# The first load of a column-mean kernel, with its 128 rows dealt to the partitions in another order

## The chip, the cores and the metric

The kernel runs on one core of one Trainium2 chip. The metric is the device time of one execution in microseconds, the median of several runs; lower is better. One profiled execution of the kernel before is at hand, with a record of each engine's instructions and of the packets that the core's 16 DMA engines moved.

## The reference

The mean over the rows of a matrix of 8192 x 8192 float32 numbers (268 MB). The result is one row of 8192 numbers.

```python
def setup_inputs():
    return {"x": np.random.randn(8192, 8192).astype(np.float32)}

def reference(x):
    return np.mean(x, axis=0)
```

## The kernel before

The 8192 rows are 64 groups of 128 rows; a group puts one row on each of the 128 partitions. They are cut into four strips of 17, 17, 15 and 15 groups (`strips`, L62). Within a strip of s groups, partition p owns the s consecutive rows that begin at row p times s of the strip. Because s is odd, a strip is s - 1 rows that are loaded in pairs, so that a partition reads 64 KB in one piece, and one row that is left, the last of the partition's s rows. The pairs stand in `pairs`, the four rows left in `singles` (L63 to L68); `rows(g)` gives one of the latter, for g from 60 to 63.

The order of the loads is written out by hand. All of them go out on one queue, SyncE's, through `load` (L51), which keeps program order. The first load is half a megabyte: columns 0 to 1023 of the row left of the first strip, 4 KB for each partition, into a small tile called `early` (L113, through `load_early`, L95). Partition p gets row 17p + 16 there. Neighbouring partitions thus read 17 rows of 32 KB apart, 544 KB, and partitions 8 apart read 4.25 MB apart.

Next come the loads of pairs, 8 MB each (`load_rows`, L73), into a ring of buffers in `bufs`: the first pair into the buffers that become the sum, then 29 more in the loop of L117. After the second turn of that loop the rest of `early`, columns 1024 to 3071 of the same 128 rows, is loaded as well (L125), again with row 17p + 16 on partition p. At the end the remaining single rows are loaded in pieces that grow smaller (L144 to L151).

VectorE adds each pair to the running sum (`add`, L78): first the two rows of a pair to one another, then that to the accumulator `acc`. The early turns add two rows at once, 16384 numbers wide. A buffer is loaded anew when the adds that read it have ended, and a no-op on ScalarE or GpSimd collects the waits ahead of an add. GpSimd adds `early` to the accumulator in two parts, in the turns of g = 24 and g = 32 (L135 to L140): columns 0 to 1023, those of the first load, and then columns 1024 to 3071.

Last, TensorE sums over the 128 partitions: a matrix product with a matrix of constants 1/8192 (`product`, L98), for the accumulator and for the rows that were never added to it, all into five PSUM banks. ScalarE and VectorE copy these out, and three small stores write the result. Since every column is summed over all partitions at the end, it doesn't matter for the sum on which partition a row stands.

Of the kernel before, what the change touches and what calls it, by code (L numbers as in the profile page):

```python
# [9 lines left out]
def kernel(  # L10
# [8 lines left out]
    P = nc.NUM_PARTITIONS  # L19
    F = 512  # L20
# [13 lines left out]
    early = sb.tile([P, E * F], f32, name="early")  # L34
# [16 lines left out]
    def load(dst, src):  # L51
        ins = tc.keep_in_program_order(nc.sync.dma_start(out=dst, in_=src)).ins  # L52
        k = len(loads)
        over = loads[k - 8:k - 6] if k >= 8 and k % 2 == 0 else []
        tc.declare_no_dep(ins, group="loads", keep=over, reason="the reader of the buffer waited")
        for o in over:
            tc.add_manual_dep(ins, o.name, sync, reason="covers the next load too")
        tc.add_to_no_dep_group("loads", ins)
        loads.append(ins)
        return ins  # L60

    strips = [17, 17, 15, 15]  # L62
# [7 lines left out]
    def rows(g):  # L70
        return singles[g - (G - 4)]

    def load_rows(g, u, n):  # L73
        return load(bufs[:, u:u + n, :], pairs[g // 2])
# [20 lines left out]
    def load_early(lo, hi):  # L95
        load(early[:, lo * F:hi * F], rows(G - 4)[:, lo * F:hi * F])
# [13 lines left out]
        )).ins  # L110

    sums2 = bufs[:, U - 2:, :]
    load_early(0, 2)  # L113
    first = [load_rows(0, U - 2, 2)]
    tc.keep_in_program_order(nc.scalar.copy(out=warm[:], in_=ones[:]))  # L115
    ahead = []
# [121 lines left out]
```

## Time and profile before

| what | value |
|---|---|
| median of 3 runs | 628.02 us (628.0 to 628.23) |
| span of the profiled execution | 626.3 us |
| data read from HBM | 268.44 MB, 429 GB/s over the span |
| VectorE busy | 527.7 us (84%), 92.2 us idle ahead of its adds |
| TensorE busy | 18.3 us (3%) |
| GpSimd busy | 7.4 us (1%) |
| SyncE's first load: issue begins, ends | 0.74 us, 1.13 us |
| VectorE's first add begins | 42.86 us |

The span runs from the first to the last instruction of the profiled execution; the time of a run is a little longer than that. SP is SyncE, DVE VectorE, ACT ScalarE, POOL GpSimd, PE TensorE; SPq is SyncE's sequencer, and L52 is line 52 of the kernel. Every load has line L52, whichever place in the kernel calls the helper, and every add L80.

A windows view gives for each stretch of time the busy time and count of PE, of its weight loads (PEld), of DVE, ACT and POOL, then the granted clock of TensorE (1.00 is full speed), the mean busy share of the 16 DMA engines, and the GB/s that they moved. The packet records of the trace give start, duration and size of each piece that a DMA engine moved; those of the first load are 128 packets of 4096 bytes, and those of the pairs 3840 packets of 65536 bytes.

### The profile page before, as it was taken

The page shows a single profiled execution, that of the slowest core. Times are in us where ns is not written, and L with a number is a line of the kernel's source. Part 1 is how long each engine was busy: PE and PEld are TensorE (multiplying, and loading weights), DVE is VectorE, ACT ScalarE, POOL GpSimd, SP SyncE. Part 2 cuts the span into 40 slices and gives each one's busy share as a digit, 9 for nine tenths or more (in the row PEclk, how much of TensorE's full clock was granted, in tenths as well). Part 3 has the DMA queues.
Part 4 walks back from the last instruction along what each step waited for, and adds up shares of the span by engine and source line. Part 5 has one row for each costly group of instructions (what it writes and reads, how often), then busy time and mean ns, then how long its engine had stood idle before and what let it go on. Part 6 is the DMA issues. An engine that isn't in the chain of part 4 may idle for free.

```text
span 626.3 us, 464 instructions
## 1 busy us (share of the span) xinstructions
PE 18.3 (3%) x120; PEld 4.6 (1%) x120; DVE 527.7 (84%) x60; ACT 3.7 (1%) x6; POOL 7.4 (1%) x8
## 2 busy tenths in 40 slices
PE   0000020000000000000000000000000000000035
PEld 0000000000000000000000000000000000000001
DVE  0028979999988998888988899988898888998895
ACT  0000000000000000000000000000000000000001
POOL 0000000000000000010000200000000000000000
PEclk9999999999999999999999999999999999999999
DMA  9999999999999999999999999999999999999997
GB/s 393 444 402 434 437 469 402 469 402 465 406 448 423 440 431 423 448 410 460 406 465 402 469 402 469 402 469 402 469 402 465 406 448 423 423 448 406 431 435 305
DMA packets 5658, 268.50 MB, mean 429 GB/s; under 512 B 636, under 2 KB 652, under 8 KB 1048
## 3 DMA queue, kind: packets, MB, share of 16 engines
q1 hardware_dynamic: 5648, 268.46, 99.2%
q8 instruction: 1, 0.02, 0.0%
q10 hardware_dynamic: 8, 0.01, 0.0%
q14 instruction: 1, 0.01, 0.0%
HBM read 268.44 MB, written 0.03 MB: 429 GB/s over the span
## 4 chain that ended last, share of the span: by engine, by line
DMA 70%; DVE 28%; PE 1%; SPq 0%; issue 0%; ACTq 0%; POOLq 0%
DMA bufs<-in_x_dram 70%; DVE bufs L80 28%; PE bank L102 1%; SPq L52 0%; ACTq L83 0%; DVE fin L192 0%; POOLq L83 0%
## 5 line engine op out<-in xcount | busy, mean ns | idle before, releaser
L80 DVE TENSOR_TENSOR bufs<-bufs 128x8192 f32<-128x8192 f32 (+4 forms) x59 | 527.4, 8939 | 92.2 <-POOLq L83 52.3
L102 PE MATMUL bank<-bufs,ones 128*32 128x512 f32 (+2 forms) x120 | 18.3, 634 | 605.0 <-DVE bufs L80 517.7
L137 POOL TENSOR_TENSOR bufs<-bufs,early 128x1024 f32<-128x1024 f32 (+1 forms) x2 | 6.8, 3416 | 350.0 <-DVE bufs L80 350.0
L102 PEld LDWEIGHTS bank<-bufs,ones 128*32 128x32 f32 x120 | 4.6, 120 | 618.5 <-issue 610.7
L182 ACT COPY bufs<-bank 128x512 f32<-128x512 f32 x3 | 1.8, 586 | 618.2 <-PE bank L102 618.2
L192 DVE COPY fin<-bank 128x128 f32<-128x128 f32 x1 | 0.3, 292 | 3.8 <-PE bank L102 3.8
L115 ACT ACT_TABLE_LOAD x1 | 1.3, 1283 | 0.7 <-PEq L222 0.7
L182 ACT COPY fin<-bank 128x384 f32<-128x384 f32 x1 | 0.5, 480 | 1.0 <-PE bank L102 1.0
L115 ACT COPY warm<-ones 128x32 f32<-128x32 f32 x1 | 0.2, 217 | 0.0
L40 POOL TENSOR_TENSOR ready<-ones 128x1 f32<-128x1 f32 x1 | 0.2, 192 | 0.1
L37 POOL MEMSET ones<- 128x32 f32 x1 | 0.1, 124 | 0.3 <-POOLq L222 0.3
L222 POOL MEMSET const-bfloat16-1.0<- 128x1 bf16 x1 | 0.1, 101 | 0.0
L222 POOL MEMSET const-uint8-127<- 128x1 uint8 x1 | 0.1, 101 | 0.0
L222 POOL MEMSET const-float32-0.0<- 128x1 f32 x1 | 0.1, 98 | 0.2 <-issue 0.2
L222 POOL MEMSET const-float32-1.0<- 128x1 f32 x1 | 0.1, 98 | 0.0
## 6 DMA issues: line engine op xcount, KB each, us to landing
bufs<-in_x_dram SPq DMA_DIRECT2D x2, 4096.0 KB, 16.7
bufs<-in_x_dram SPq DMA_DIRECT2D x1, 2560.0 KB
bufs<-in_x_dram SPq DMA_DIRECT2D x1, 2048.0 KB, 21.3
early<-in_x_dram SPq DMA_DIRECT2D x1, 1024.0 KB, 62.0
bufs<-in_x_dram SPq DMA_DIRECT2D x1, 1024.0 KB, 23.2
bufs<-in_x_dram SPq DMA_DIRECT2D x1, 768.0 KB, 24.7
early<-in_x_dram SPq DMA_DIRECT2D x1, 512.0 KB
bufs<-in_x_dram SPq DMA_DIRECT2D x30, 29.9
```

Of the source, the lines that this page charges most:

```text
L37: nc.gpsimd.memset(ones[:], 1.0 / M)
L40: nc.gpsimd.tensor_add(out=ready[:], in0=ones[:, 0:1], in1=ones[:, 1:2]))
L80: ins = tc.keep_in_program_order(nc.vector.tensor_add(out=dst, in0=a, in1=b)).ins
L102: return tc.keep_in_program_order(nc.tensor.matmul(out=dst, lhsT=ones[:], rhs=cols, start=start, stop=stop, tile_position=(0, 32 * q), ski ...
L115: tc.keep_in_program_order(nc.scalar.copy(out=warm[:], in_=ones[:]))
L137: ins = tc.keep_in_program_order(nc.gpsimd.tensor_add(out=acc[:, cols], in0=acc[:, cols], in1=early[:, cols])).ins
L182: return tc.keep_in_program_order(nc.scalar.copy(out=dst, in_=src)).ins
L192: ended = nc.vector.tensor_copy(out=fin[:, 3 * W:], in_=banks[4][:, :W]).ins
L222: nc = _bacc.Bacc("TRN2", target_bir_lowering=False, num_devices=1)
```

## The change

The first load takes the same columns of the same 128 rows, and its destination is the same; the order of the rows over the partitions is another. The rows of the strip are seen as 8 blocks (k) of 16 (e) times 17 (s), and the source of the load runs over e first and k second. Partition 8e + k, which had row 17(8e + k) + 16, now has row 17(16k + e) + 16. Neighbouring partitions then read 8.5 MB apart, 16 x 544 KB, and partitions 8 apart read 544 KB apart. If an engine serves 8 partitions one after the other, the 16 engines are at rows 544 KB apart at one time, and before at rows 4.25 MB apart. The second part of `early`, `load_early(2, E)`, is as it was.

```diff
     sums2 = bufs[:, U - 2:, :]
-    load_early(0, 2)
+    s = strips[0]
+    spread = x[:s * P, :].rearrange("(k e s) c -> s e k c", k=8, s=s)[s - 1]
+    load(early[:, :2 * F], spread[:, :, :2 * F])
     first = [load_rows(0, U - 2, 2)]
```

## The prediction

> **What bounds the kernel now.** I read the page first (span, DMA slices, chain of waits), then the windows view of the first microseconds, where the changed load runs, and last the window of the long middle. The page:
>
> ```profile
> span 626.3 us, 464 instructions
> DMA  9999999999999999999999999999999999999997
> ...
> q1 hardware_dynamic: 5648, 268.46, 99.2%
> ...
> DMA 70%; DVE 28%; PE 1%; SPq 0%; issue 0%; ACTq 0%; POOLq 0%
> ...
> bufs<-in_x_dram SPq DMA_DIRECT2D x30, 29.9
> ```
>
> The reader is to see that one queue, q1, keeps the 16 DMA engines at work for 99.2% of the span. VectorE stands in the chain with 28%, but section 1 of the page has it 84% busy: it follows the loads, they don't follow it. The last line says that a usual load lands 29.9 us after its issue. Such a load is 8.39 MB, which at the 432 GB/s of the middle (next fence) is 19.4 us, so it is issued some 10.5 us before its turn comes. A stream that is some tenths of a microsecond earlier or later therefore finds its issues ready, and VectorE, idle for 92.2 us in all, can follow it.
>
> The windows view; the columns that count are the last two, the DMA share and GB/s. A packet is booked whole in the window in which it starts, so shares can pass 1:
>
> ```profile
> 1.50:1.75 0.25, 0.00 (x0) 0.00 (x0) 0.00 (x0) 0.25 (x1) 0.00 (x0) 1.00 0.00 0
> 1.75:2.00 0.25, 0.00 (x0) 0.00 (x0) 0.00 (x0) 0.25 (x1) 0.00 (x0) 1.00 1.07 197
> 2.00:2.25 0.25, 0.00 (x0) 0.00 (x0) 0.00 (x0) 0.23 (x2) 0.00 (x0) 1.00 0.94 147
> 2.25:2.50 0.25, 0.00 (x0) 0.00 (x0) 0.00 (x0) 0.00 (x0) 0.00 (x0) 1.00 0.41 131
> 2.50:2.75 0.25, 0.00 (x0) 0.00 (x0) 0.00 (x0) 0.00 (x0) 0.00 (x0) 1.00 0.94 377
> 2.75:3.00 0.25, 0.00 (x0) 0.00 (x0) 0.00 (x0) 0.00 (x0) 0.00 (x0) 1.00 0.95 393
> ...
> 3.80:620.00 616.20, 14.95 (x76) 3.50 (x80) 527.38 (x59) 0.59 (x1) 6.83 (x2) 1.00 1.00 432
> ```
>
> So there is a dry stretch up to about 1.8 us, a slow start of the first load, 0.5 to 0.75 us long, and then a full stream to the end: share 1.00 from 3.80 to 620. Nothing that happens to the first load is hidden: the engines go from it straight to the next loads, and what it gains or loses moves all behind it.
>
> **The changed load now.** It is 128 rows of 4 KB, 0.52 MB, 8 packets for each of 16 engines. Packets in a window are GB/s times 0.25 us over 4096 bytes, and their time is share times 0.25 us times 16. From 1.75 to 2.50 these are 12 + 9 + 8 = 29 packets with (1.07 + 0.94 + 0.41) x 4 = 9.68 us, or 334 ns each. From 2.50 to 3.00 they are 23 + 24 = 47 packets with 1.89 x 4 = 7.56 us, 161 ns each; the trace's packet records give 159 ns for nearly all of them. The excess of the start is 9.68 - 29 x 0.159 = 5.07 us over 16 engines, **0.32 us** for each. The rows have the same distance, 4.25 MB, in the slow and in the fast part. So distance alone doesn't slow a packet; what is special at the start is that 16 engines begin within some 0.1 us of one another. In the records, 24 of the first packets took 160 to 681 ns with a mean of 374, and afterwards the engines are out of step, entering the next load between 3.39 and 3.79 us.
>
> **The change part by part.** (1) *Same work.* One load of 128 rows of 4 KB is replaced by one of the same rows. No instruction is added, removed or moved; the early tile holds the rows in another order of partitions, and each of its columns is summed over all partitions anyway. Cost of everything behind it (the GpSimd adds of 4.49 and 2.34 us, the matrix products, the last stores): nothing, as no shape and no wait differs. The GpSimd adds are at 276 and 353 us, far from the start, so no cover of theirs is touched.
>
> (2) *The slow start.* If rows 544 KB apart don't get in each other's way in the first step, the 0.32 us go; the first round of the following 64 KB packets took 2463 ns in the mean against 2422 for the rest, another 0.04 us that may go with it. Upper end of the gain: 0.36 us. Lower end: no gain, if the slow packets are what the engines' first reads cost from any rows; and below that a loss, if 544 KB is the worse distance, bounded by the same excess again, +0.32 us. The nearest row is the fast part of the same load, which shows that reads of this very kind run at 159 ns when they don't begin together, so something in the beginning together is avoidable; but nothing in the trace says that distance cures it. I take two thirds of the 0.32: **-0.21 us**.
>
> [...]
>
> (3) *Issue.* SP's first DMA instruction took 0.39 us (0.74 to 1.13) and the first packet followed 0.64 us later, at 1.77. Its source now has three dimensions instead of two. Loads of two dimensions take 0.33 to 0.44 us on SP; SP's stores with three dimensions 0.54 and 0.70. So the issue changes by -0.06 (0.33 - 0.39) to +0.31 us (0.70 - 0.39), all on the path, because the engines are dry until then; the three loads behind it on SP start later by as much, but their packets wait for this load's anyway. It is nearest to the other loads into 128 partitions: **+0.05 us**.
>
> Sum: -0.21 + 0.05 = -0.16, said as -0.2. Against the profiled execution: 626.3 - 0.2 = 626.1 us of span. The median of the runs shown, 628.02, is 1.7 us above the span, time before the first and after the last instruction that the change doesn't touch, so 628.02 - 0.2 = **627.8 us**. With the ends of both terms: -0.36 - 0.06 = -0.42 (627.6) to +0.32 + 0.31 = +0.63 (628.65).
>
> **The rivals.** *A: nothing comes of it.* The slow first packets are the price of engines that begin cold, or the engines stay in step longer and meet in the 64 KB packets of the next load instead (the worst of that first round took 2553 ns, 0.13 us more than the rest). For it: the load is fast at 4.25 MB from 2.50 us on. Against it: the first packets spread from 160 to 681 ns, like engines that queue for one thing. Time 628.0 to 628.2.
>
> *B: the rows are dealt to the engines badly* (slower). The load's two sides are now cut differently, 16 x 8 rows on one, 128 partitions on the other. If two engines write through one way into the on-chip memory, or only 8 engines get the work, the load needs the time of 16 packets in a row where it has 8: 8 x 0.159 = 1.27 us, on the path since all that follows queues behind the last engine, and with the +0.05 of the issue 1.3 us: 629.3. It decides as soon as the deal isn't one block of 8 partitions to each engine on a way of its own. For it: the stream is bound by the engines (share 1.00), so an unequal deal can't be caught up. Against it: the outermost sizes, 16 and 128, both divide by 16. If only one engine got the rows it would be 120 x 0.159 = 19 us, 647.
>
> [...] No row of this trace shows which partitions an engine has.
>
> *C: it gains more than its own load* (faster beyond the bound below). The 3840 packets of 64 KB take 2422.5 ns in the mean and 2415 at best; were the engines in a better phase for the whole run, 240 x 7.5 ns = 1.8 us of each engine would go, with 0.3 at the start 2.1 us: 625.9. Against it: the phases drift during the run (the middle stretches stand at 2418 to 2430 ns), so the start doesn't fix them.
>
> **How the numbers follow.** A measurement of this kernel can tell about 0.2%, 1.26 us, from no change: faster is below 626.8, slower above 629.3. Forecast 0.46 and A 0.26, both within 0.2%; B 0.21, of which most lies at the bound or above it; C 0.07. So faster 0.07, same 0.73, slower 0.20. The likeliest case's own range is 627.6 to 628.65. The range, 627.2 to 629.4, goes on downwards for part of C and upwards to B with eight engines or shared ways, and leaves out one engine alone and the rest of C.
>
> **What would show it.** Right: packets of the first load at about 160 to 220 ns from the start, so 1.75 to 2.50 us carries clearly more than 158 GB/s on the mean, the engines enter the next load nearer to 3.2 than to 3.57 us (their mean now), and the window 3.80 to 620 stays at 432 GB/s. A: the same low GB/s up to 2.50, or a first round of 64 KB packets over 2463 ns. Issue: SP's first instruction longer than 0.39 us and a first packet after 1.77. B: packets of the first load near 318 ns to its end, or engines that enter the next load 1.3 us apart. C: a middle above 432 GB/s. The prediction is wrong if the time leaves 627.6 to 628.65, and its reason is wrong if the start is as slow as before.

## The result, and the profile after

| | median | runs | span of the profiled execution |
|---|---|---|---|
| before | 628.23 us | 21 (627.93 to 628.81) | 626.3 us |
| changed | 629.21 us | 21 (628.83 to 629.51) | 627.5 us |

The ratio is 1.0014, with a 95% interval of 1.0008 to 1.0019: the change makes the kernel **slower**, by 0.98 us (0.16%) in the medians. That is inside the wide range, 627.2 to 629.4 us, whose upper end was set for rival B, and within 0.2% of no change. But it is on the other side of no change than the forecast, and outside the 627.6 to 628.65 us beyond which the prediction called itself wrong.

The page of the changed kernel, the same lines as of before:

```profile
span 627.5 us, 464 instructions
DMA  9999999999999999999999999999999999999997
...
q1 hardware_dynamic: 5648, 268.46, 99.2%
...
DMA 70%; DVE 28%; PE 1%; SPq 0%; issue 0%; ACTq 0%; POOLq 0%
```

On this scale nothing has changed: the same packets, the same queue busy for 99.2%, the same chain. Whatever was lost stands in stretches too short for the page. The timeline of SyncE's queue (start, duration, what) shows the first part of it:

```profile
0.74 0.70 SPq L52 DMA_DIRECT2D early<-in_x_dram  x1
1.50 1.52 SPq L52 DMA_DIRECT2D bufs<-in_x_dram  x3
```

The first load's issue takes 0.70 us where it took 0.39. The windows of the changed kernel's start (the columns as before: TensorE's clock, DMA share and GB/s come last, and a packet is booked where it starts) show the rest:

```profile
1.75:2.00 0.25, 0.00 (x0) 0.00 (x0) 0.00 (x0) 0.25 (x1) 0.00 (x0) 1.00 0.00 0
2.00:2.25 0.25, 0.00 (x0) 0.00 (x0) 0.00 (x0) 0.24 (x2) 0.00 (x0) 1.00 0.18 33
2.25:2.50 0.25, 0.00 (x0) 0.00 (x0) 0.00 (x0) 0.00 (x0) 0.00 (x0) 1.00 1.14 213
2.50:2.75 0.25, 0.00 (x0) 0.00 (x0) 0.00 (x0) 0.00 (x0) 0.00 (x0) 1.00 0.67 197
2.75:3.00 0.25, 0.00 (x0) 0.00 (x0) 0.00 (x0) 0.00 (x0) 0.00 (x0) 1.00 1.08 295
3.00:3.25 0.25, 0.00 (x0) 0.00 (x0) 0.00 (x0) 0.00 (x0) 0.00 (x0) 1.00 0.86 295
3.25:3.50 0.25, 0.00 (x0) 0.00 (x0) 0.00 (x0) 0.00 (x0) 0.00 (x0) 1.00 0.82 295
3.50:3.75 0.25, 0.00 (x0) 0.00 (x0) 0.00 (x0) 0.00 (x0) 0.00 (x0) 1.00 1.02 344
3.75:4.00 0.25, 0.00 (x0) 0.00 (x0) 0.00 (x0) 0.00 (x0) 0.00 (x0) 1.00 1.25 328
4.00:4.25 0.25, 0.00 (x0) 0.00 (x0) 0.00 (x0) 0.00 (x0) 0.00 (x0) 1.00 7.53 2441
4.25:4.50 0.25, 0.00 (x0) 0.00 (x0) 0.00 (x0) 0.00 (x0) 0.00 (x0) 1.00 3.90 1327
4.50:4.75 0.25, 0.00 (x0) 0.00 (x0) 0.00 (x0) 0.00 (x0) 0.00 (x0) 1.00 1.50 524
...
3.80:620.00 616.20, 14.78 (x67) 3.30 (x71) 526.62 (x59) 0.00 (x0) 6.83 (x2) 0.58 1.00 433
```

Three things are to be seen. The first packet comes at 2.22 us (1.77 before). The load then never reaches the 377 and 393 GB/s that it had before from 2.50 us on: it moves 197, three times 295, 344 and 328 up to 4.00. And the next load's first 64 KB packets, those that start from 4.00 to 4.75, are long: (7.53 + 3.90 + 1.50) x 4 = 51.7 us, less six packets of 4 KB at about 0.31, is 49.9 us over 16 packets, 3.1 us each, where one takes 2.42. The middle of the run is as before, 433 against 432 GB/s. TensorE's granted clock is 0.58 there against 1.00. It isn't the cause: one of the plain controls below had 0.58 too and stood within 0.04% of before, and TensorE works for 19.3 us in all.

In the packet records a loss can be summed. Two numbers tell it: the time that the small load's packets take beyond 159 ns each, over 16 engines, and the mean time beyond 2420 ns of the first 64 KB packet that each engine takes behind them.

| us for each engine | first packet at | excess of 4 KB packets | excess of next 64 KB packet | sum of both |
|---|---|---|---|---|
| before | 1.77 | 0.32 | 0.04 | 0.37 |
| changed | 2.22 | 0.60 | 0.68 | 1.28 |

So 0.45 us are lost ahead of the first packet and 0.91 in the packets, 1.36 in all. By the packet records the changed kernel has its first 9 MB 1.37 us later than before, which agrees; at the last packet of x it is 1.16 us, and the medians differ by 0.98. The 0.2 to 0.4 us that disappear on the way are taken for chance of one execution: in the profile of before the 64 KB packets between 78 and 156 us took 2429.5 ns in the mean, in the profile after 2421.5, and in three plain runs below 2419.5 to 2420.8; 32 packets of each engine, 8 ns longer, are 0.26 us. The profiled execution of the changed kernel was also the longest of its 21, at 629.51 us.

### The profile page after: what moved, and what is told of

It reads as the page before. It is cut to its first block, busy times and chain, and to the rows that moved or that the text cites. A ratio compares the mean times of both kernels' runs of the same rounds, so it can differ in the third digit from the quotient of the medians.

```text
span 627.5 us, 464 instructions
## 1 busy us (share of the span) xinstructions
PE 19.3 (3%) x120; PEld 4.8 (1%) x120; DVE 527.7 (84%) x60; ACT 3.7 (1%) x6; POOL 7.3 (1%) x8
## 3 DMA queue, kind: packets, MB, share of 16 engines
q1 hardware_dynamic: 5648, 268.46, 99.2%
## 4 chain that ended last, share of the span: by engine, by line
DMA 70%; DVE 28%; PE 1%; SPq 0%; issue 0%; ACTq 0%; POOLq 0%
DMA bufs<-in_x_dram 70%; DVE bufs L80 28%; PE bank L102 1%; SPq L52 0%; ACTq L83 0%; DVE fin L194 0%; POOLq L83 0%
## 5 line engine op out<-in xcount | busy, mean ns | idle before, releaser
L80 DVE TENSOR_TENSOR bufs<-bufs 128x8192 f32<-128x8192 f32 (+4 forms) x59 | 527.4, 8939 | 93.4 <-POOLq L83 53.9
L102 PE MATMUL bank<-bufs,ones 128*32 128x512 f32 (+2 forms) x120 | 19.3, 652 | 605.2 <-DVE bufs L80 517.4
L40 POOL TENSOR_TENSOR ready<-ones 128x1 f32<-128x1 f32 x1 | 0.2, 193 | 0.1
```

The source lines that it names most:

```text
L40: nc.gpsimd.tensor_add(out=ready[:], in0=ones[:, 0:1], in1=ones[:, 1:2]))
L80: ins = tc.keep_in_program_order(nc.vector.tensor_add(out=dst, in0=a, in1=b)).ins
L102: return tc.keep_in_program_order(nc.tensor.matmul(out=dst, lhsT=ones[:], rhs=cols, start=start, stop=stop, tile_position=(0, 32 * q), ski ...
```

## The experiments

The theory after this look: the cost comes from how the load is cut, not from where its rows lie. The cut is the sizes in which the source of a load is given: the changed one has an outermost size of 16, with 8 rows in each, and the destination has 128 partitions. The rivals: the 544 KB distance itself is bad; the slow first round is chance; the longer issue explains everything. No record here shows which partitions an engine has: where the expectations speak of an engine's block of partitions, of groups, or of ways into the partitions, that is the author's theory. All comparisons below are with the kernel before, run on the same chip beside them. The chip differs between groups of runs (the kernel before took 628.23 to 628.46 us), so two experiments are held against each other by their distances from it. The profile numbers are of one execution each.

**The changed kernel once more.**

> The changed kernel once more, so that its profile can be held against the first one: the first load's issue took 0.70 us on SP (0.39 before), the first packet stood at 2.22 us (1.77 before), and the first 64 KB packet of each engine took 3099 ns in the mean (2463 before). Theory (a three-dimensional source costs issue time and, through it, time): issue again 0.70 and first packet again 2.2, time 0.14% above before. Theory 2 (the slow first 64 KB round belongs to the change too): again near 3.1 us. Rival (that round is chance of one execution): between 2.4 and 2.6 us this time.

Measured 629.3 against 628.25 us, ratio 1.0014 (1.0005 to 1.0023). Issue 0.70 us, first packet at 2.22, excess 0.63 in the 4 KB packets, and a first 64 KB round of 2748 ns, 0.33 us more than 2420; the sum is 0.96. The round lies between the two values that were set, 3.1 us and 2.4 to 2.6. It is read here as part of the change, with a size that varies from one execution to the next (0.68 and 0.33); the next run has 0.33 again.

**Three dimensions at the old distance.**

```diff
-    load_early(0, 2)
+    far = x[:17 * P, :].rearrange("(e r) c -> e r c", r=136)[:, 16:136:16, :]
+    load(early[:, :2 * F], far[:, :, :2 * F])
```

> The first load has a source of three dimensions, 16 blocks of 8 rows, but each engine's block lies 4.25 MB from the next one's, as before; inside a block the rows are 512 KB apart. It reads 128 other rows of the strip in place of the right ones, the same bytes. If the source's dimensions are what costs: issue 0.70 us, first packet at 2.2 us, time 0.1 to 0.16% above before, as with the change. If the 544 KB distance costs and the dimensions don't: issue 0.39, time as before within 0.04%. If both: half of the way, with the first 64 KB round near 2.46 us and the issue at 0.70.

629.23 us, ratio 1.0013 (1.0004 to 1.0022), the whole cost of the change: issue 0.70, first packet at 2.22, excess 0.64 and 0.33 us. The nearness of the rows has no part in it.

**Two dimensions with near pieces.**

```diff
-    load_early(0, 2)
+    near = x[:272, :].rearrange("r c -> (r c)").rearrange("(p f) -> p f", p=P)
+    load(early[:, :2 * F], near[:, :2 * F])
```

> The first load has a source of two dimensions, 128 pieces of 4 KB that are 68 KB apart, so that partitions 8 apart read 544 KB apart; the pieces are other parts of x than the right ones, the same bytes. If the dimensions cost and the distance doesn't: issue 0.39 us, first packet at 1.77, time as before or, if the nearness relieves the first packets as the prediction had it, 0.03 to 0.05% below. If the distance costs: issue 0.39, but packets of the first load with a mean excess of 0.6 us per engine as in the change (0.32 before) and a first 64 KB round near 3.1 us, time about 0.1% above before.

628.29 us, ratio 0.9999 (0.9990 to 1.0008): no cost. Issue 0.39, first packet at 1.75. The excess is 0.44 and 0.07 us, not less than before's 0.32 and 0.04, so there is no sign of the relief either. A load whose partitions 8 apart read 544 KB apart thus gains nothing.

**The dealt load second, behind the first pair.** The edit is against the changed kernel.

```diff
-    load(early[:, :2 * F], spread[:, :, :2 * F])
     first = [load_rows(0, U - 2, 2)]
+    load(early[:, :2 * F], spread[:, :, :2 * F])
```

> The dealt load is issued second, behind the first pair of rows (8 MB), so that its longer issue stands behind other transfers. If the cost of the change is issue and cold start of the first load: the first packet (64 KB now) at 1.75 us or earlier, time no worse than before, 0 to 0.1% below, since the 0.31 us of issue and the slow 4 KB start are covered. If dealing the rows costs wherever it stands (engines sharing ways, a bad phase): time 0.05 to 0.15% above before.

629.69 against 628.25 us, ratio 1.0021 (1.0012 to 1.0030). The issue (0.69 us, from 1.18 us on) is covered there, as the load's packets pass at 22 us, and the small load doesn't meet the cold start, and it costs still more. This was the run that decided, with its control:

**The plain load second.** Lines L113 and L114 of the kernel before change places.

> The first two loads change places as in the run with the dealt load second, but the small load has its plain source of two dimensions. It is the control for that run, where the 4 KB packets went at 159 ns until 22.15 us and at 240 to 390 after, in the middle of the stream. If a badly shared way into the partitions is the cause (theory): all 128 packets here at 159 to 170 ns, the 64 KB packets behind them at 2420, and 1.2 us (0.19%) less than with the dealt load second; time about 628.4, the rest being the cold start with 64 KB packets. If small packets between large ones are slow by themselves (rival): again 250 ns and 629.7 us.

628.52 against 628.36 us, ratio 1.0004 (0.9995 to 1.0013). The windows of both where the small load passes, around 22 to 24 us, the run with the dealt load first:

```profile
22.00:22.50 0.50, 0.00 (x0) 0.00 (x0) 0.00 (x0) 0.00 (x0) 0.00 (x0) 1.00 1.22 336
22.50:23.00 0.50, 0.00 (x0) 0.00 (x0) 0.00 (x0) 0.00 (x0) 0.00 (x0) 1.00 0.95 197
23.00:23.50 0.50, 0.00 (x0) 0.00 (x0) 0.00 (x0) 0.00 (x0) 0.00 (x0) 1.00 1.03 262
```

and its plain control:

```profile
22.00:22.50 0.50, 0.00 (x0) 0.00 (x0) 0.00 (x0) 0.00 (x0) 0.00 (x0) 1.00 1.06 434
22.50:23.00 0.50, 0.00 (x0) 0.00 (x0) 0.00 (x0) 0.00 (x0) 0.00 (x0) 1.00 1.30 541
23.00:23.50 0.50, 0.00 (x0) 0.00 (x0) 0.00 (x0) 0.00 (x0) 0.00 (x0) 1.00 4.81 2073
```

At a DMA share of about 1, the dealt load moves 197 and 262 GB/s in the second and third window, the plain one 434 in the first (in the third, and partly in the second, its engines are already starting 64 KB packets). In the records, all 128 packets of the control took 159 ns. Those of the dealt load took 159 ns until 22.15 us, the first 26 of the 128, and then up to 392. From 22.2 to 23.4 us 16 to 18 of them are in flight at a time by the records, and the DMA share is about 1: all 16 engines work on the load, and each packet takes longer. Its excess is 0.79 us in these and 0.48 us in the 64 KB packets behind them, together **1.27 us** for each engine. That is just 8 packets x 0.159 us: as if the 0.52 MB went at half rate, with the backlog worked off in the packets that follow. In time the dealt load stands 1.44 us above the kernel before and the plain one 0.16 us, each on its own chip: 1.28 us apart.

**The kernel before, started late.**

```diff
+    landed(readied)
     load_early(0, 2)
```

Here `readied` is the small GpSimd addition of L40.

> The kernel before, but SP waits with the first load until GpSimd's second small instruction has ended (1.13 us), so that the issue begins about 0.42 us later. What a later start of the stream costs: if all of it passes to the end, first packet at 2.2 us and +0.42 us, 0.07%. If the issue's delay is the whole of the change's cost (rival): 0.13 to 0.15%, as the change. If a later start is partly caught up: below 0.05%.

628.63 against 628.36 us, ratio 1.0004 (0.9995 to 1.0012). The issue began at 1.16, the first packet came at 2.17, and the first 9 MB were there 0.40 us later than before. At the last packet of x it was 0.18 us. The time is 0.27 us longer, with an interval that has both no change and the whole 0.42 us in it; 0.04% is under the 0.05% that was set for a start that is partly caught up. So the medians can't tell how much of a late start passes on. Its ratio stays below the change's 1.0014, though the intervals overlap.

**Three dimensions with 128 outermost.**

```diff
-    load_early(0, 2)
+    apart = rows(G - 4).rearrange("p (j w) -> p j w", w=F)[:, 0:4:2, :]
+    load(early[:, :2 * F].rearrange("p (j w) -> p j w", w=F), apart)
```

> The first load's source has three dimensions again, but the outermost has 128 entries: each partition gets two pieces of 2 KB from its own row (the second one 2 KB further on than in the kernel before, so 512 of the early columns hold other data). Theory (what costs is the cut of the outermost dimension into 16, which hands an engine 8 partitions in a row): packets of 2 KB at 84 ns after the start, a first 64 KB round near 2.46 us; only the longer issue remains if it belongs to three dimensions as such (0.70 us, +0.3 to +0.45 us) and 0.07 us for the smaller packets, so 0.01 to 0.08% above before. Rival (three dimensions cost, however they are cut): 0.13 to 0.16% above before with a first round of 2.7 us or more.

628.45 us, ratio 1.0002 (0.9993 to 1.0011). The issue took 0.45 us, neither 0.39 nor 0.70, the 2 KB packets 84 ns once started, the first 64 KB round 2453. So a third dimension behind the 128 is worth 0.06 us of issue here; the rest came with the cut of the outermost one.

**Two halves of 64 partitions, first.**

```diff
-    load_early(0, 2)
+    tc.keep_in_program_order(nc.sync.dma_start(
+        out=early[:64, :2 * F], in_=rows(G - 4)[:64, :2 * F]))
+    load(early[64:, :2 * F], rows(G - 4)[64:, :2 * F])
```

> The first load in two, rows for partitions 0 to 63 and for 64 to 127, each plain and of two dimensions; the same bytes in the same places. Each half is dealt to 16 engines with 4 partitions, so if two engines meet at one way into the memory whenever a load covers too few different groups of partitions (theory), the packets slow to 240 to 320 ns, together with the first 64 KB round up to 1.27 us are lost for each engine, and the time is 0.1 to 0.2% above before, without any third dimension. Rival (dimensions alone): packets at 159 ns after the start and a time within 0.03% of before, the second issue being covered by the first half's packets.

631.06 us, ratio 1.0043 (1.0031 to 1.0056): a cost without a third dimension, but twice what the theory gave. In the records the excess is 0.63 us in the 4 KB packets, 0.50 in the next round and 0.48 in the round after that, and four of the engines began their first 64 KB packet only at 5.2 to 5.9 us, after 12 others at 3.7 to 4.5. Why these four waited isn't settled, and with it a part of the 2.70 us. Since the cold start is mixed in here, the halves were tried again in the middle of the stream, below.

**The second part dealt, twice the bytes.**

```diff
-                load_early(2, E)
+                s = strips[0]
+                spread = x[:s * P, :].rearrange("(k e s) c -> s e k c", k=8, s=s)[s - 1]
+                load(early[:, 2 * F:], spread[:, :, 2 * F:E * F])
```

> The first load is plain, and the second part of the early rows (1 MB, 8 KB for each partition, at about 61 us, in the middle of the stream) is dealt in 16 x 8 instead. If the deal halves the rate of the bytes that it covers (theory): 8 packets of 309 ns twice as long, 2.47 us for each engine, and 0.35 to 0.42% above before. If the cost is a fixed one of the dealt load, or belongs to the cold start (rival): 0 to 0.2%.

630.72 against 628.23 us, 2.49 us more (0.40%) where 2.47 were worked out; ratio 1.0047 (1.0035 to 1.0058), which is above the 0.35 to 0.42% that was expected: one of the six runs took 633.21 us, the others 630.57 to 630.93. Windows of that run where its dealt megabyte passes, far from any start:

```profile
61.90:62.40 0.50, 0.00 (x0) 0.00 (x0) 0.00 (x0) 0.00 (x0) 0.00 (x0) 1.00 1.16 246
62.40:62.90 0.50, 0.00 (x0) 0.00 (x0) 0.00 (x0) 0.00 (x0) 0.00 (x0) 1.00 1.00 213
62.90:63.40 0.50, 0.00 (x0) 0.00 (x0) 0.41 (x1) 0.00 (x0) 0.00 (x0) 1.00 1.00 213
```

and of the kernel before, where the same megabyte is plain:

```profile
61.90:62.40 0.50, 0.00 (x0) 0.00 (x0) 0.17 (x1) 0.00 (x0) 0.00 (x0) 1.00 0.89 377
62.40:62.90 0.50, 0.00 (x0) 0.00 (x0) 0.50 (x1) 0.00 (x0) 0.00 (x0) 1.00 1.18 492
```

213 GB/s at a share of 1.00 is half of the stream's 433. The cost grows with the bytes (2.49 us for 1.05 MB, 1.28 us for 0.52) and needs no cold start.

**Other cuts, second in the queue.** The same rows in 32 x 4 and in 64 x 2: `k=8` becomes `k=4` and `k=2`, in the place where 16 x 8 cost 1.28 us.

> As the run with the dealt load second, but dealt in 32 x 4: the source's outermost dimension has 32 entries. With 16 x 8 that run stood 1.2 us above its plain control, with 128 at none. If any outermost size below 128 hands an engine 8 partitions in a row: again 1.2 us above the control (629.7). If the engines are chosen by groups of four partitions, 32 groups are what that needs: 159 ns packets and the control's time (628.5).

> The same with 64 x 2. If any outermost size below 128 costs: about 629.7. If the cost falls with the size (theory of groups of four): no more than 32 x 4 does, 628.5.

628.39 us, ratio 1.0002 (0.9993 to 1.0011), and 628.33 us, 1.0003 (0.9994 to 1.0011). In both every one of the 128 packets took 159 ns. The windows of 32 x 4, where 16 x 8 moved 336 and 197 GB/s:

```profile
22.00:22.50 0.50, 0.00 (x0) 0.00 (x0) 0.00 (x0) 0.00 (x0) 0.00 (x0) 1.00 0.94 385
22.50:23.00 0.50, 0.00 (x0) 0.00 (x0) 0.00 (x0) 0.00 (x0) 0.00 (x0) 1.00 1.32 549
```

Their issue still took 0.67 us, covered in that place. So the longer issue comes with each of these three cuts (0.69 us with 16 x 8), and the half rate with 16 x 8 alone.

**Two halves of 64 partitions, second.** The two plain half loads of above, behind the first pair.

> The small load stands second and is plain, but goes out in two loads of 64 partitions each. If the engines meet at shared ways into the partitions (theory), 64 partitions have half of the ways: packets at 159 ns for the first two or three of each engine, then 240 to 390, and 1.27 us above the plain control of that place, 629.6 to 629.9. If only the cut of the source matters (rival): 159 ns throughout, 628.5.

629.77 against 628.23 us, ratio 1.0024 (1.0014 to 1.0033): 1.54 us above the kernel before, where the plain control of that place is 0.16 above it. One window, where the control moved 541 GB/s:

```profile
22.50:23.00 0.50, 0.00 (x0) 0.00 (x0) 0.00 (x0) 0.00 (x0) 0.00 (x0) 1.00 0.97 205
```

The packets go at 159 ns at first and take 243 in the mean of all 128; the excess is 0.67 and 0.46 us. With no third dimension and the rows in their old order the picture is that of the dealt load. No record shows what the two have in common that the fast cuts lack; that it is the partitions that are written at one time is a reading.

**The better cuts, first.** The change itself with `k=4` and with `k=2`. Left open until here was whether the order of the right rows relieves the cold start once the cut costs nothing.

> The change with 32 x 4 in place of 16 x 8: the dealt load is the first one again, but cut so that its packets ran at 159 ns in the middle of the stream. What is left is the longer issue and what the order of the rows does to the cold start. If the order relieves the start (the prediction's step): excess of the first load's packets well under the 0.32 us per engine of before, below 0.15, first packet at 2.2 us, time 0 to 0.03% above before. If it doesn't: excess 0.3 to 0.45 us, time 0.04 to 0.09% above before, as with the late first load.

> The same with 64 x 2, another order of the same rows. If the order of the rows matters for the cold start, excess and time differ from the 32 x 4 run by more than 0.15 us; if the start costs the same from any rows, both stand at 0.3 to 0.45 us of excess and 0.04 to 0.09% above before.

628.74 against 628.46 us, ratio 1.0004 (0.9995 to 1.0013), and 628.92, ratio 1.0007 (0.9998 to 1.0016). The windows of the run with 32 x 4:

```profile
2.00:2.25 0.25, 0.00 (x0) 0.00 (x0) 0.00 (x0) 0.23 (x2) 0.00 (x0) 1.00 0.86 82
2.25:2.50 0.25, 0.00 (x0) 0.00 (x0) 0.00 (x0) 0.00 (x0) 0.00 (x0) 1.00 1.81 164
2.50:2.75 0.25, 0.00 (x0) 0.00 (x0) 0.00 (x0) 0.00 (x0) 0.00 (x0) 1.00 0.14 16
...
3.50:3.75 0.25, 0.00 (x0) 0.00 (x0) 0.00 (x0) 0.00 (x0) 0.00 (x0) 1.00 0.99 410
```

The slow packets are there: the 23 slowest took 582 ns in the mean, longer than the 23 slowest of before with 383. From 3.50 us it runs at full rate, with a first 64 KB round of 2427 ns. The excess is 0.61 us with 32 x 4 and 0.75 with 64 x 2, against 0.32 in the profile of before and 0.37 to 0.44 in the three other plain first loads of 4 KB packets. That is also above the 0.3 to 0.45 us that was expected if nothing is relieved. Neither order relieves the start. That one is worse than another is seen in single executions alone, and the intervals of the times don't separate it.

## Why the prediction was wrong, point by point

**What bounds the kernel: right.** The stream stands at a share of 1.00, and what a load loses reaches the end: the dealt megabyte came out as +2.49 us where 2.47 had gone in. For the late start alone, +0.27 us where 0.42 had gone in, the times can't tell.

**Same work, nothing behind it: right.** The middle has 433 GB/s and the adds 527.4 us, as before.

**The slow start, -0.21 us: this step failed, in sign too.** It read the 0.32 us of excess as engines in each other's way at rows 4.25 MB apart, and took two thirds of it as curable by distance; and its sum had no term for the new cut of the load, which stood in rival B alone. The runs showed no effect of the distance: 4.25 MB with the new cut costs the whole 0.13%, pieces 68 KB apart with the old cut nothing, and the right rows in two other orders have an excess of 0.61 and 0.75 us. The remark that the fast part of the same load has the same distance was the evidence against this step, and was passed over. In place of the gain, the packets lost 0.91 us more than before in the one profile of the change and 0.59 in the other. With the 0.37 us that the cold start took in the profile of before that is 1.28 and 0.96 us in all, near the 1.27 of the middle of the stream; that the two losses overlap is a reading, not shown. Two smaller readings were off as well: the first 24 packets took 371 ns in the mean, not 374, and the first 13, all of which began before one had ended, began over 0.23 us, not within 0.1.

**Issue, +0.05 us: mis-sized.** It was 0.31 us in the issue and another 0.14 between its end and the first packet (0.78 us where it was 0.64), 0.45 together. The nearest row was not the loads into 128 partitions but SP's store of 0.70 us, the upper bound that was named. The third dimension alone is 0.06 us; as first or second load, a source whose outermost size isn't the destination's 128 took 0.67 to 0.70 us.

**Rival B: right, and given too little.** Its price was 8 x 0.159 = 1.27 us, and measured in the middle of the stream it was 1.27 us. That its time, 629.3, is so near the 629.21 that the kernel took is partly luck: as a difference it was 1.3 us where 0.98 was measured, the median of before was 628.23 and not 628.02, and an issue that cost 0.40 us more than forecast made up for packets that lost less at the start. Of its two forms, the one with only 8 engines at work is excluded by the 16 and more packets in flight at a time; left, as a reading, is the one in which all 16 work and get in each other's way. What spoke against it, that 16 and 128 both divide by 16, fits the 16 to 18 packets in flight, but the load went at half rate all the same.

Which partitions an engine has, and where engines would meet, is in no profile and no record here. What the runs show is which loads are slow: 16 x 8 goes at half rate (213 GB/s), and two loads of 64 partitions are slow again with an excess of 1.13 us, where 32 x 4 and 64 x 2 take 159 ns a packet. That engines meet on their way into the partitions is a reading that none of these runs contradicts, not one that a record shows.

**Rival A** had the cold start right, as far as it goes: it stayed in the other orders that were run (excess 0.61 us with 32 x 4, 0.75 with 64 x 2, 0.44 in the 4 KB packets of the near pieces). It left the price of the cut out. Its sign, a first round of 64 KB packets over 2463 ns, was seen in the profile of the change (3099), while B's packets near 318 ns were not (234 in the mean of the 128): that profile alone could not tell the two apart, and the pair of runs with the small load second did. **Rival C** fell: the middle of the run didn't move (433 against 432 GB/s).

None of the runs is below the kernel before; the nearest, the near pieces with 628.29 us, can't be told from it.

## What to carry to other kernels

In these runs the shape of a load's source was part of its cost even with the same bytes, packets and destination (0.98 us for the change): keep the outermost dimension at the 128 partitions, or, behind another load, a cut as fine as 32 (159 ns a packet), since 16 x 8 moved its bytes at half rate here (213 against 433 GB/s) and two halves of 64 partitions nearly so (an excess of 1.13 us against 1.27). As first load the finer cuts weren't shown to be free either: they stood 0.28 and 0.46 us above the kernel before, within the noise. On a kernel whose DMA engines are never idle (a share of 1.00 here), price such a load at its bytes over the halved rate (2.47 us worked out so, 2.49 measured), and look for it in the packets behind it as well, where a third or more of the loss stood (0.48 of 1.27 us, 0.46 of 1.13). A slow stretch at the start isn't explained by the one thing about it that an edit can change; hold it against a stretch with the same property that is fast.

## What was not expected of the hardware

The loss is booked late: with the deal at half rate, the first 26 of 128 packets still took 159 ns, and 0.48 us of the 1.27 stood in 64 KB packets of another, plain load. SP's issue of the small load, as first or second, went by how its sides are cut: 0.39 to 0.41 us for 128 rows, 0.45 with a third dimension behind the 128, 0.57 to 0.63 for 64 partitions, 0.67 to 0.70 for an outermost source size of 16, 32 or 64. The cut isn't all: the load of a pair right behind took 0.41 to 0.44 us after a plain small load and 0.57 to 0.66 after a dealt or halved one, and the second part of `early`, plain in all runs but one, took anything from 0.43 to 0.71 us, with no reason that these runs show. And the cold start has a size of its own: in the runs with 64 KB packets first, these took 3.16 to 3.23 us instead of 2.42, a loss of 0.74 to 0.81 us, where with the plain small load in front it was 0.37 to 0.51 (both excesses together). In time the two places of the plain load differ by 0.16 us in the medians, which these runs can't tell from nothing.
